# First norm on turned rows, triangular inverses through cleared images in DRAM, and a last token tile in two column halves: one encoder layer on one core

## The chip, the core and the metric

The kernel runs on one core of one Trainium2 chip. A core has a matrix engine (TensorE, PE in the profile; its weight loads are PEld), VectorE (DVE), ScalarE (ACT), GpSimd (POOL) and SyncE (SP). In this kernel SP issues every DMA, in one queue and in order; 16 DMA engines carry the transfers. The metric is the time of one execution in microseconds on the device. The kernel is written in Python against a planner: each engine's instructions are put in an order at build time, by the order of the program, by priorities, and by the planner's own estimates of when an operand will be there. Semaphores are placed from the data dependences. On the chip each engine then runs its list in that order.

## The reference

One layer of an encoder on 1024 tokens of width 1024, in float32:

```python
h = _rms_norm(x, g_mix_pre[l])
proj = h @ w_in[l]
aq, ak, av, dqkv, dgate, dalpha, dbeta = jnp.split(proj, IN_SPLITS, axis=-1)
attn_o = _window_attention(aq, ak, av, attn_sink[l])            # after rotary on aq, ak
dn_o = _gated_deltanet(dqkv, dgate, dalpha, dbeta, conv_w[l], a_log[l], dt_bias[l], g_dn_out[l])
mix = jnp.concatenate([attn_o, dn_o], axis=-1) @ w_out[l]
x = x + _rms_norm(mix, g_mix_post[l])
c = _memory_cross_attention(_rms_norm(x, g_cross_pre[l]), _rms_norm(mem, g_mem[l]), w_cq[l], w_ckv[l], w_co[l])
x = x + _rms_norm(c, g_cross_post[l])
f = _swiglu(_rms_norm(x, g_ffn_pre[l]), w_gate_up[l], w_down[l])
x = x + _rms_norm(f, g_ffn_post[l])
```

`_rms_norm` is `x * rsqrt(mean(x * x) + EPS) * gain`. In the delta net, for each of four heads and two directions, the sequence is cut into chunks; in each chunk a unit lower triangular system is solved (`triangular_solve(tmat, rhs)`, with `tmat = lower + I` from products of keys), and a scan over the chunks carries a 128x128 state.

## The kernel before

All products are done with float32 split into two parts `hi` and `lo` (`split`, L100: a cast on ScalarE, L103, and a subtraction, L104), three matmuls for each 128x128 block of weight.

**Start.** The token tiles `xts` (128 tokens each) are loaded, six of eight at first, with the gain `gmix` repeated over 128 partitions (L209) and the identity. For each tile: sum of squares on ScalarE (L222), the root by a power on POOL (`rstd_of`, L159 to L163), scaling by root and gain on VectorE (L225), eight 128x128 transposes on TensorE into two PSUM tiles (L230), and `split` of each into `hhi`, `hlo` (L232). A half of 512 tokens (`hT[hf]`) consists of four tiles. The weights of the first two projections (`ws`, L295) are asked for behind tile 1 and tile 3. `gemm_b` (L257) then does the two key projections, half by half (L297 to L300). Then come the decays' small projection (`wab`), the convolutions (L277) and the stages of `ORDER_1`, `ORDER_2` and `ORDER_3`, three lists that give the order of the program by letters: `k`, `q`, `v` are projections, `E`, `K`, `U`, `C` products of a head, `B0`, `B1` the base inverses of a group of two heads, `L0` to `L3` the levels of a head, `A`, `V`, `G` projections for attention and gates, `W` attention windows, `s01` a step of both scans.

**Base inverses and levels.** A chunk pair of 128 rows has a 128x128 triangular matrix, in four diagonal blocks of 32. `base_inverse(g)` (L521) inverts all 32x32 blocks of a group at once, one block per partition (128 partitions: 2 directions, 2 heads, 8 pairs, 4 blocks), with 60 small instructions on VectorE (L545, L547). The inverse, scaled in two ways (`A` and `V`), goes to `d_inv` (L554, four stores per group of 64 partitions, 4 KB each). `levels(h)` (L557) puts the 32x32 inverses together to inverses of 64 and 128. It loads the blocks four times as columns of blocks (`cz`, `cw`, L565), makes copies with parts of both on POOL (`m5`, `c5`, `c6`, L575 to L578), and expands these columns on VectorE to matrices that are zero outside the diagonal blocks (`D5`, `D6`, `Z0`, `Z1`, L588, a product with the mask `dmask`). `part(b)` does four pairs; both parts of a head run interleaved (`together`). The matmuls are L604 and L610, the results are stored from `Z` to `d_pz` (L629), where the scan reads them.

**End.** The last product of the feed-forward part goes over four token tiles `t` (L1774): two loads of turned activations (`atr`, L1779), their split, 33 matmuls of 512 columns into `X[t]` (L1784), an addition (L1791), sum of squares on ScalarE (`sq_of`, L1706), the root by a power on POOL (`rstd_at`, L1718 to L1723), scaling plus residual on VectorE for two column halves `za` and `zv` (L1796), and a store of each (L1797).

Of the kernel before, what the change touches and what calls it, by code (L numbers as in the profile page):

```python
# [10 lines left out]
F32 = mybir.dt.float32  # L11
# [25 lines left out]
ORDER_1 = ("k0 k1 E0 K0 U0 E1 K1 U1 S0 q0 v0 q1 C0 v1 E2 C1 k2 E3 k3 q2 K2 U2 v2 K3 U3 S1 q3 C2 v3 C3 B0 B1").split()  # L37
# [39 lines left out]
def tile_hybrid_block(  # L77
# [16 lines left out]
    def f32(ap):  # L94
        return ap.bitcast(F32)
# [69 lines left out]

    gain_at = {"cross": 60, "mem": 60 + KT, "ffn": 60 + 2 * KT}
# [16 lines left out]
    d_inv = [[dram.tile([2, 2, NT, 4, 32, 32], F32, name=f"d_inv{g}{i}") for i in range(2)] for g in range(2)]  # L183
# [19 lines left out]
    xts = [t1.tile([P, D], F32, tag="xt", name="xt", bufs=6) for _ in range(6)]  # L203
    gmix = t1.tile([P, D], F32, tag="gmix", name="gmix", bufs=1)
    xload = []
    for t in range(6):
        xload.append(nc.sync.dma_start(xts[t], x[t * P:(t + 1) * P, :]))
        if t == 0:
            nc.sync.dma_start(gmix, g_mix_pre[0].partition_broadcast(P))  # L209
            nc.sync.dma_start(ident, consts[:, 0:P])  # L210
    hT = []
    for hf in range(2):
        hi = hx.tile([P, KT, HALF], F32R, name=f"hhi{hf}")
        lo = hx.tile([P, KT, HALF], F32R, name=f"hlo{hf}")
        for j in range(4):
            t = 4 * hf + j
            xt = xts[t] if t < 6 else t1.tile([P, D], F32, tag="xt", name="xt", bufs=6)
            if t >= 6:
                nc.sync.dma_start(xt, x[t * P:(t + 1) * P, :])
# [4 lines left out]
            rstd_of(rs, ss, 1.0 / D, EPS)  # L224
            nc.vector.scalar_tensor_tensor(xt, xt, rs, gmix, ALU.mult, ALU.mult)  # L225
            for kq in range(2):
                pt = small()
                for k in range(4):
                    c = (4 * kq + k) * P
                    nc.tensor.transpose(pt[:, k * P:(k + 1) * P], xt[:, c:c + P], ident)  # L230
                o = slice(4 * kq, 4 * kq + 4), slice(j * P, (j + 1) * P)
                split(hi[:, o[0], o[1]], lo[:, o[0], o[1]], pt.rearrange("p (k t) -> p k t", k=4))  # L232
# [15 lines left out]
    nc.vector.tensor_copy(mU_r, cm["mU"])  # L248
    nc.vector.tensor_copy(mL_r, cm["mL"])
# [4 lines left out]
    nc.scalar.activation(nega, prm[:, 0:8], AF.Exp)  # L254
# [40 lines left out]
    ws = [load_w(dcols(1, h), KT, P, after=xload[t]) for h, t in ((0, 1), (1, 3))]  # L295
# [12 lines left out]
    nc.vector.tensor_scalar(wabr, hT[0][0].bitcast(F32)[:, :, 0:P], 0.0, None, ALU.mult)  # L308
# [105 lines left out]
    dmask = sm.tile([P, 4, 32], F32, name="dmask")  # L414
    nc.gpsimd.memset(dmask, 0.0)
    for q in range(4):
        nc.gpsimd.memset(dmask[32 * q:32 * q + 32, q, :], 1.0)
# [103 lines left out]
    def base_inverse(g):  # L521
# [30 lines left out]
        for i in range(2):  # L552
            for d in range(2):
                nc.sync.dma_start(d_inv[g][i][d].rearrange("h c b r s -> (h c b) r s"),  # L554
                                  (A if i == d else V)[64 * d:64 * d + 64])

    def levels(h):  # L557
# [6 lines left out]
        def fetch(dst, i, d):  # L564
            nc.sync.dma_start(dst, d_inv[g][i][d, hh].rearrange("c b r s -> (b r) c s"))  # L565

        cz = [blocks("cz0"), blocks("cz1")]
        cw = [blocks("cw0"), blocks("cw1")]
        m5, c5, c6 = blocks("m5"), blocks("c5"), blocks("c6")
        for d in range(2):  # L570
            fetch(cz[d], 1, d)
            fetch(cw[d], 0, d)
        for q in range(4):
            r = slice(32 * q, 32 * q + 32)
            nc.gpsimd.tensor_copy(m5[r], cz[1 - q % 2][r])  # L575
            nc.gpsimd.tensor_copy(c5[r], cw[q % 2][r])
        for d in range(2):
            nc.gpsimd.tensor_copy(c6[64 * d:64 * d + 64], cw[d][64 * d:64 * d + 64])  # L578
        def part(b):
# [5 lines left out]
            L5, L6, D5, D6 = wide("L5"), wide("L6"), wide("D5"), wide("D6")  # L585
            Z = [wide("Z0"), wide("Z1")]
            for e, dst, src in ((nc.vector, D5, c5), (nc.vector, D6, c6), (nc.vector, Z[0], cz[0]), (nc.vector, Z[1], cz[1])):
                e.tensor_tensor(dst.rearrange("p c (q n) -> p c q n", q=4), bc(src[:, c4, :], 2, (P, 4, 4, 32)),  # L588
                                        bc(dmask, 1, (P, 4, 4, 32)), ALU.mult)
# [24 lines left out]
            z5 = tl_.tile([P, 4, 32], F32, tag="z5", name="z5", bufs=2)  # L614
# [5 lines left out]
            mov6 = tl_.tile([P, 4, 64], F32, tag="mov6", name="mov6", bufs=2)  # L620
# [109 lines left out]
    def issue(order, table):  # L730
        for o in order:
            table[o[0]](*(int(c) for c in o[1:]))

    issue(ORDER_1, {**{n: delta_proj(n) for n in "kqv"}, "E": decays, "K": turned_keys, "U": key_products, "S": beta_rows,
                    "C": query_products, "B": base_inverse})
    pp_.close()
# [967 lines left out]
    def sq_of(src, t, ch):  # L1704
        jk = tp_.tile([P, 512], F32, tag="jk", name="jk", bufs=1)
        nc.scalar.activation(jk, src, AF.Square, accum_out=sq[:, ch, t:t + 1])  # L1706
# [63 lines left out]
    for t in range(4):  # L1770
        nc.vector.tensor_tensor(za[:, t], za[:, t], X[t], ALU.add)
        sq_of(za[:, t], 4 + t, 1)

    for t in range(4):  # L1774
        tt = slice(t * P, (t + 1) * P)
        for k0, n in ((0, 6), (6, 5)):
# [53 lines left out]
```

## Time and profile before

| | |
|---|---|
| median of 3 runs | 1531.19 us (1529.92 to 1532.13) |
| the profiled execution | 1531.03 us |
| its span from first to last instruction | 1529.3 us |
| mean granted clock of TensorE over the span | 0.994 |
| instructions | 21202 |
| DMA | 261.06 MB, 275159 packets, of them 34904 under 512 bytes |
| matmuls | 7403 |

The page gives, in this order, busy time by engine, the span in 40 slices of 38 us (one digit each, in tenths), DMA queues, the chain of work that ended last, and groups of instructions by line. In a line of a group, `out<-in x8 | 10.2, 1281 | 9.4 <-POOL rs` means 8 instructions, 10.2 us busy in all, 1281 ns each, and 9.4 us in which the engine stood idle just before them, mostly until POOL's `rs`. Lines of the view in order of time begin with start and duration in microseconds. Matmuls overlap in the pipeline, so the distance from one to the next, about 0.23 us for 512 columns, is shorter than the duration shown.

### The profile page before, as it was taken

Reading aid. Unit: us, or ns where it says so; the run is one execution under the profiler, and the core shown is the slowest. Engines: PE = TensorE matmul, PEld = TensorE weight load, DVE = VectorE, ACT = ScalarE, POOL = GpSimd, SP = SyncE. Lnnn points to the kernel's source line nnn. Section 1 sums busy time; section 2 is a strip of 40 time slices with the busy share of each in tenths; the row PEclk is TensorE's granted clock in tenths of the full one; section 3 lists DMA queues with packets and bytes.
Section 4 is the critical chain, followed back from the end, with each engine's and each line's share of the span. In section 5 each row is a group of like instructions: output and inputs, shape, how many; then the busy total and the mean of one; then the engine's idle time right before and its main releaser. Section 6 shows DMA issues by size and latency. Waiting matters only on the chain.

```text
span 1529.3 us, 21202 instructions
## 1 busy us (share of the span) xinstructions
PE 1475.7 (96%) x7403; PEld 1239.1 (81%) x7403; DVE 1116.3 (73%) x1805; ACT 752.0 (49%) x1541; POOL 364.1 (24%) x369
## 2 busy tenths in 40 slices
PE   6999999998999999999999999999999999999997
PEld 5888888877889778888788877888888888888786
DVE  6868999787888866538567768676867774696665
ACT  5578821447557764455544685223222332454532
POOL 2020221311226203252201002433534342000021
PEclk9999999999999999999999999999999999999999
DMA  6235575856987584458725554343434333853355
GB/s 208 76 109 148 144 194 142 218 176 173 322 279 236 186 296 152 141 167 271 241 97 173 192 182 134 97 138 116 146 109 153 124 103 111 321 208 97 104 177 167
DMA packets 275159, 261.06 MB, mean 171 GB/s; under 512 B 34904, under 2 KB 206829, under 8 KB 275053
## 3 DMA queue, kind: packets, MB, share of 16 engines
q1 hardware_dynamic: 275053, 259.71, 53.9%
q8 instruction: 58, 0.95, 0.3%
q14 instruction: 48, 0.39, 0.1%
HBM read 181.25 MB, written 75.79 MB: 168 GB/s over the span
## 4 chain that ended last, share of the span: by engine, by line
PE 61%; DVE 10%; DMA 10%; ACT 4%; issue 3%; SPq 2%; POOL 1%; DVEq 0%; POOLq 0%; ACTq 0%
PE pD L1481 7%; PE pE L1481 7%; PE pA L1481 6%; PE pmg L1071 6%; PE pdX L1687 6%; PE pst L1287 5%; PE pcq L262 4%; PE pB L1481 3%; PE psc L810 2%; PE pdA L1687 2%; PE pdD L1687 2%; PE pg L262 2%; DMA wraw<-in_w_gate_up_dram 1%; PE pco L1186 1%; PE pdX L1784 1%
## 5 line engine op out<-in xcount | busy, mean ns | idle before, releaser
L103 ACT CAST whi<-wraw 128x1024 fp32r<-128x1024 f32 x96 | 100.8, 1051 | 133.0 <-DMA wraw<-in_w_gate_up_dram 37.0
L262 PE MATMUL pg<-hlo,whi 128*128 128x512 f32 x352 | 139.1, 396 | 0.0
L262 PE MATMUL pg<-hhi,whi 128*128 128x512 f32 x352 | 139.1, 396 | 0.0
L262 PE MATMUL pg<-hhi,wlo 128*128 128x512 f32 x352 | 138.1, 393 | 0.0
L104 POOL TENSOR_TENSOR wlo<-wraw,whi 128x1024 fp32r<-128x1024 f32 x36 | 88.3, 2453 | 189.6 <-ACT whi L103 188.2
L1481 PE MATMUL pA<-b,whi 128*128 128x512 f32 x352 | 111.9, 400 | 3.6 <-ACT m L1508 2.8
L104 DVE TENSOR_TENSOR wlo<-wraw,whi 128x1024 fp32r<-128x1024 f32 x60 | 76.0, 1269 | 46.0 <-ACT whi L103 42.4
L1481 PEld LDWEIGHTS pA<-b,whi 128*128 128x128 f32 x352 | 66.5, 192 | 19.2 <-ACT m L1508 4.0
L1687 PE MATMUL pdX<-dhl,whi 128*128 128x512 f32 x264 | 76.1, 390 | 1.5 <-ACT dhl L103 0.8
L262 PEld LDWEIGHTS pg<-hhi,whi 128*128 128x128 f32 x352 | 66.3, 189 | 13.4 <-ACT hhi L103 0.2
L262 PEld LDWEIGHTS pg<-hhi,wlo 128*128 128x128 f32 x352 | 66.2, 188 | 12.8
L262 PEld LDWEIGHTS pg<-hlo,whi 128*128 128x128 f32 x352 | 66.2, 188 | 12.7
L1564 POOL TENSOR_TENSOR act<-act,up 128x512 f32<-128x512 f32 x33 | 50.7, 1538 | 83.1 <-DVE up L1563 61.8
L1481 PE MATMUL pA<-b,wlo 128*128 128x512 f32 x176 | 69.9, 398 | 0.5 <-DVE wlo L104 0.5
L103 ACT CAST whi<-araw 128x1024 fp32r<-128x1024 f32 (+1 forms) x36 | 35.3, 982 | 67.9 <-PE pdX L1687 27.6
L104 DVE TENSOR_TENSOR wlo<-araw,whi 128x1024 fp32r<-128x1024 f32 (+1 forms) x36 | 40.9, 1135 | 36.1 <-ACT whi L103 35.7
L1536 POOL TENSOR_TENSOR sr<-wraw 128x512 f32<-128x512 f32 x22 | 30.3, 1379 | 150.7 <-DMA wraw<-in_w_gate_up_dram 98.7
L287 DVE SCALAR_TENSOR_TENSOR acc<-cp,cols,acc 128x1024 f32<-128x1024 f32 x48 | 62.1, 1297 | 0.1
L1687 PEld LDWEIGHTS pdX<-dhl,whi 128*128 128x128 f32 x264 | 49.3, 188 | 12.7 <-ACT dhl L103 1.1
L1721 POOL TENSOR_SCALAR frs<-sq 128x1 f32<-128x1 f32 x8 | 11.9, 1497 | 194.5 <-ACT jk L1706 193.6
L103 ACT CAST dhl<-b 128x512 fp32r<-128x512 f32 x66 | 40.3, 620 | 31.6 <-PE pdA L1687 13.7
L1481 PE MATMUL pB<-s0h,s1h 128*128 128x512 f32 x176 | 54.5, 391 | 0.0
(484 smaller groups left out, 4285.5 us busy)
## 6 DMA issues: line engine op xcount, KB each, us to landing
wraw<-in_w_gate_up_dram SPq DMA_DIRECT2D x54, 512.0 KB, 3.9
kv<-d_kv SPq DMA_DIRECT2D x32, 512.0 KB, 7.5
wraw<-in_w_in_dram SPq DMA_DIRECT2D x22, 512.0 KB, 4.2
b<-in_w_down_dram SPq DMA_DIRECT2D x20, 512.0 KB, 8.0
araw<-d_as SPq DMA_DIRECT2D x20, 512.0 KB, 3.7
pz<-d_pz SPq DMA_DIRECT2D x32, 256.0 KB, 7.6
wraw<-in_w_ckv_dram SPq DMA_DIRECT2D x16, 512.0 KB, 6.3
wraw<-in_w_out_dram SPq DMA_DIRECT2D x16, 512.0 KB, 3.7
```

The lines of the kernel that those rows point to most:

```text
L103: nc.scalar.copy(hi, src)
L104: return (eng or nc.vector).tensor_tensor(lo, src, f32(hi), ALU.subtract)
L262: nc.tensor.matmul(p_, w[:, k, :], ah[a][:, k, :], start=(k == 0 and i == 0), stop=(k == nk - 1 and i == 2))
L287: nc.vector.scalar_tensor_tensor(acc, cp[:, t:t + S], taps[t], acc, ALU.mult, ALU.add)
L810: nc.tensor.matmul(out[:, d, h, :], lt[:, d, h, :], rt[:, d, h, :], start=True, stop=True)
L1071: nc.tensor.matmul(pp[t], act[a][:, k, tt], w_[:, kk, :], start=(k == 0 and i == 0), stop=(k == KT - 1 and i == 2))
L1186: nc.tensor.matmul(po, vr_[a][:, kt, cs], pts[kt][b_], start=(kt == 0 and i == 0), stop=(kt == 1 and i == 2))
L1287: nc.tensor.matmul(bank, a[:, tt], w, start=(start and i == 0), stop=(stop and i == 2), skip_group_check=not check)
L1481: nc.tensor.matmul(out_, w[a][:, k, :], xx[b_][:, k, :], start=(start and k == 0 and i == 0), stop=(k == HK - 1 and i == 2), skip_group_ch ...
L1536: nc.gpsimd.tensor_tensor(s[0], b_[:, 0:HK], b_[:, HK:], ALU.add)
L1564: nc.gpsimd.tensor_tensor(o_, o_, up, ALU.mult)
L1687: nc.tensor.matmul(banks[t], a[:, k - k0, tt], w, start=(first and k == 0 and i == 0), stop=(k == NB - 1 and i == 2), skip_group_check=not ...
```

## The change

Three parts, independent of each other.

1. The gain is loaded as 8 rows of 128 (4 KB), turned once on TensorE to a column per block (`gcol`), and multiplied where the turned block is cast (ScalarE, by `scale=g`) and cut (VectorE). Scaling of a token tile is by its root alone. All eight token tiles have buffers of their own and are loaded first; the first two weights are queued on SP behind tile 3, their casts and subtractions behind tile 3's root and scaling, and behind the sixth turned block. A PSUM tile now holds one block column `k` of four token tiles instead of four columns of one. Roots are a Sqrt on ScalarE and a reciprocal on VectorE, its table loaded at the start by `warm`. Some small copies and the Exp for `nega` are queued behind the last scaling and the last root.
2. `d_inv` is replaced by `d_lv`, for each group an image of 16 matrices of 128 rows by 512 columns (four matrices side by side: `D5`, `D6`, `Z0`, `Z1`). It is cleared from a tile of zeros by four DMAs of 1 MB per group, at the letters `Z` in `ORDER_1`; `base_inverse` stores its blocks on the diagonals, and `levels` loads four images at once (1 MB, `DZ`, three buffers). `m5` goes through a small tensor `d_m5`. The columns, copies, masks and expansions go. `z5` and `mov6` get one buffer instead of two.
3. Roots of the last four tiles are on ScalarE and VectorE too. The last tile's 33 matmuls of 512 columns become 33 of the first 256 columns and 33 of the last 256, the latter in a PSUM tile of their own; additions, squares and stores follow by halves.

```diff
-ORDER_1 = ("k0 k1 E0 K0 U0 E1 K1 U1 S0 q0 v0 q1 C0 v1 E2 C1 ...
+ORDER_1 = ("k0 k1 Z E0 Z K0 Z U0 Z E1 K1 U1 S0 q0 Z v0 Z q1 Z C0 Z v1 E2 C1 ...
+    def inverse_root(rs, ss, scale, bias):
+        root = nc.scalar.activation(rs, ss, AF.Sqrt, bias=bias, scale=scale)
+        nc.vector.reciprocal(rs, rs)
+        return root
-    d_inv = [[dram.tile([2, 2, NT, 4, 32, 32], F32, name=f"d_inv{g}{i}") for i in range(2)] for g in range(2)]
+    LW, LB_ = 4 * P, 32 * 4 * P + 32
+    d_lv = [dram.tile([1, 8 * NT * LB_ + LW], F32, name=f"d_lv{g}") for g in range(2)]
+    d_m5 = [dram.tile([8 * NT, 32, 32], F32, name=f"d_m5{g}") for g in range(2)]
+    def diagonal(g, kind):
+        at = kind * P
+        return (d_lv[g][0, at:at + 8 * NT * LB_].rearrange("(n y) -> n y", y=LB_)[:, 0:32 * LW]
+                .rearrange("n (r w) -> n r w", w=LW)[:, :, 0:32])
+    def level_rows(g, x0):
+        return (d_lv[g][0, 0:8 * NT * LB_].rearrange("(x y) -> x y", y=4 * LB_)[x0:x0 + 4, 0:P * LW]
+                .rearrange("x (p w) -> p x w", w=LW))
...
-    xts = [t1.tile([P, D], F32, tag="xt", name="xt", bufs=6) for _ in range(6)]
-    gmix = t1.tile([P, D], F32, tag="gmix", name="gmix", bufs=1)
+    xts = [t1.tile([P, D], F32, tag="xt", name="xt", bufs=NT) for _ in range(NT)]
+    grow = t1.tile([KT, P], F32, tag="grow", name="grow", bufs=1)
+    gcol = t1.tile([P, KT], F32, tag="gcol", name="gcol", bufs=1)
...
-            nc.sync.dma_start(gmix, g_mix_pre[0].partition_broadcast(P))
+            nc.sync.dma_start(grow, g_mix_pre[0].rearrange("(c p) -> c p", p=P))
             nc.sync.dma_start(ident, consts[:, 0:P])
+    warm = t1.tile([P, 1], F32, tag="ss", name="warm", bufs=4)
+    nc.scalar.activation(warm, epsc, AF.Sqrt)
+    pt = small()
+    nc.tensor.transpose(pt[:, 0:KT], grow, ident[0:KT, 0:KT])
+    nc.vector.tensor_copy(gcol, pt[:, 0:KT])
...
-            rstd_of(rs, ss, 1.0 / D, EPS)
-            nc.vector.scalar_tensor_tensor(xt, xt, rs, gmix, ALU.mult, ALU.mult)
-            for kq in range(2):
...
+            rooted = inverse_root(rs, ss, 1.0 / D, epsc)
+            scaled = nc.vector.tensor_scalar(xt, xt, rs, None, ALU.mult)
+        if hf == 0:
+            ready.append((rooted, scaled))
+        for k in range(KT):
+            pt = small()
+            for j in range(4):
+                nc.tensor.transpose(pt[:, j * P:(j + 1) * P], xts[4 * hf + j][:, k * P:(k + 1) * P], ident)
+            g = gcol[:, k:k + 1]
+            cast = nc.scalar.activation(hi[:, k, :], pt, AF.Identity, scale=g)
+            cut = nc.vector.scalar_tensor_tensor(lo[:, k, :], pt, g, f32(hi[:, k, :]), ALU.mult, ALU.subtract)
+            if hf == 0 and k == 5:
+                ready.append((cast, cut))
...
-    ws = [load_w(dcols(1, h), KT, P, after=xload[t]) for h, t in ((0, 1), (1, 3))]
+    ws = []
+    for h in range(2):
+        with tc.issue_after(ready[h][0].ins), tc.issue_after(ready[h][1].ins):
+            ws.append(load_w(dcols(1, h), KT, P, after=xload[3]))
...
+    def clear():
+        g, x0 = cleared[0] // 4, 4 * (cleared[0] % 4)
+        cleared[0] += 1
+        nc.sync.dma_start(level_rows(g, x0), bc(zero, 1, (P, 4, LW)))
...
-        for i in range(2):
-            for d in range(2):
-                nc.sync.dma_start(d_inv[g][i][d].rearrange("h c b r s -> (h c b) r s"),
-                                  (A if i == d else V)[64 * d:64 * d + 64])
+        for d in range(2):
+            first, second = (A, V) if d == 0 else (V, A)
+            lo_, hi_ = 64 * d, 64 * d + 64
+            nc.sync.dma_start(d_m5[g][1 - d::2], second[lo_ + 1 - d:hi_:2])
+            nc.sync.dma_start(diagonal(g, 0)[d::2], first[lo_ + d:hi_:2])
+            nc.sync.dma_start(diagonal(g, 2 + d), second[lo_:hi_])
+            for q in (2 * d, 2 * d + 1):
+                nc.sync.dma_start(diagonal(g, 1)[q::4], first[lo_ + q:hi_:4])
...
+        m5 = blocks("m5")
+        nc.sync.dma_start(m5, d_m5[g][32 * hh:32 * hh + 32].rearrange("(c b) r s -> (b r) c s", b=4))
...
-            L5, L6, D5, D6 = wide("L5"), wide("L6"), wide("D5"), wide("D6")
-            Z = [wide("Z0"), wide("Z1")]
-            for e, dst, src in ((nc.vector, D5, c5), (nc.vector, D6, c6), (nc.vector, Z[0], cz[0]), (nc.vector, Z[1], cz[1])):
-                e.tensor_tensor(dst.rearrange("p c (q n) -> p c q n", q=4), bc(src[:, c4, :], 2, (P, 4, 4, 32)),
-                                        bc(dmask, 1, (P, 4, 4, 32)), ALU.mult)
+            L5, L6 = wide("L5"), wide("L6")
+            DZ = tl_.tile([P, 4, 4, P], F32, tag="DZ", name="DZ", bufs=3)
+            nc.sync.dma_start(DZ.rearrange("p c k n -> p c (k n)"), level_rows(g, hh * NT + 4 * b))
+            D5, D6, Z = DZ[:, :, 0], DZ[:, :, 1], [DZ[:, :, 2 + d] for d in range(2)]
...
+    nc.vector.tensor_tensor(zv[:, 3, 256:], zv[:, 3, 256:], X[3][:, 256:], ALU.add)
+    XL = bank("pdY")
...
+        columns = [(slice(0, 512), X[t])] if t < 3 else [(slice(0, 256), X[t][:, 0:256]), (slice(256, 512), XL[:, 0:256])]
+        for c_, p_ in columns:
+            fresh = c_.start > 0
+            for k, (ah, al) in enumerate(tiles):
                 for i, (a, w) in enumerate(((ah, t4h), (ah, t4l), (al, t4h))):
+                    nc.tensor.matmul(p_, a, w[:, k, c_], start=(fresh and k == 0 and i == 0), stop=(k == NB - 1 and i == 2),
+                                     skip_group_check=not fresh)
...
+        known = sq[:, 1, r:r + 1]
+        nc.vector.tensor_scalar(known, known, D * EPS, None, ALU.add)
+        for c_, p_ in columns:
+            nc.vector.tensor_tensor(zv[:, t, c_], zv[:, t, c_], p_, ALU.add)
+            sq_of(zv[:, t, c_], r, 0)
+            nc.vector.tensor_tensor(zv[:, t, c_], zv[:, t, c_], gp[:, c_], ALU.mult)
+            if c_.stop < 512:
+                nc.vector.tensor_tensor(known, known, sq[:, 0, r:r + 1], ALU.add)
+        rs = tp_.tile([P, 1], F32, tag="frs", name="frs")
+        inverse_root(rs, sq[:, 0, r:r + 1], 1.0, known)
+        for z, o_, c_ in [(za, 512, slice(0, 512))] + [(zv, 0, c_) for c_, _ in columns]:
+            at = slice(o_ + c_.start, o_ + c_.stop)
+            nc.vector.scalar_tensor_tensor(z[:, t, c_], z[:, t, c_], rs, xr[:, at], ALU.mult, ALU.add)
+            nc.sync.dma_start(out[there(r), at], z[:, t, c_])
```

70 lines of the change are left out of this document (21 added, 49 removed).

## The prediction

> **What bounds the kernel now.** I read the page's first two parts and its chain first, then busy time by stretch, then the first 30 us and the last 10 us in order of time, and last the groups of the operations that the change touches.
>
> ```profile
> PE 1475.7 (96%) x7403; PEld 1239.1 (81%) x7403; DVE 1116.3 (73%) x1805; ACT 752.0 (49%) x1541; POOL 364.1 (24%) x369
> PE   6999999998999999999999999999999999999997
> PE 61%; DVE 10%; DMA 10%; ACT 4%; issue 3%; SPq 2%; POOL 1%; DVEq 0%; POOLq 0%; ACTq 0%
> ```
>
> TensorE is the bound: it stands below 9 tenths in the first slice, the last one, and one slice near 345 us. The change takes no matmul away (it adds one small transpose and splits 33 others in two), so it can win only where TensorE stands still. How much that is:
>
> ```profile
> 0.00:8.00 8.00, 0.00 (x0) 0.00 (x0) 1.28 (x1) 2.43 (x3) 2.04 (x20) 1.00 0.78 239
> 8.00:24.70 16.70, 10.85 (x50) 8.44 (x50) 14.02 (x18) 13.85 (x25) 8.32 (x12) 1.00 0.82 266
> 24.70:47.80 23.10, 23.10 (x113) 19.31 (x112) 15.99 (x28) 11.33 (x19) 0.74 (x2) 1.00 0.28 81
> ...
> 180.00:220.00 40.00, 40.00 (x211) 34.02 (x209) 39.02 (x59) 15.06 (x47) 8.39 (x9) 1.00 0.64 164
> 220.00:260.00 40.00, 37.60 (x205) 31.35 (x204) 36.90 (x79) 8.11 (x18) 11.49 (x20) 1.00 0.65 159
> 260.00:300.00 40.00, 38.98 (x211) 32.93 (x211) 27.99 (x54) 13.30 (x27) 12.51 (x21) 1.00 0.84 220
> 300.00:340.00 40.00, 38.59 (x222) 32.80 (x219) 33.96 (x78) 20.60 (x54) 6.37 (x9) 1.00 0.66 188
> 340.00:400.00 60.00, 53.45 (x364) 47.71 (x363) 43.87 (x120) 39.10 (x86) 10.03 (x12) 1.00 0.72 214
> ```
>
> Columns: stretch, its length, busy us and count of PE, PEld, DVE, ACT, POOL, clock, DMA share, GB/s. PE has nothing for 8 us, half a load until 24.7 us, and then no gap (47.86, quoted below, is the last matmul of the first two projections). From 180 to 400 us, where the levels and the start of the scan lie, it is idle 0 + 2.40 + 1.02 + 1.41 + 6.55 = 11.4 us in all, with VectorE close to full in the first two stretches. These are the three places: start, levels, tail.
>
> **Part 1, the first norm.** What it is now, in order of time and by groups:
>
> ```profile
> 1.24 0.42 SPq L209 DMA_DIRECT2D gmix<-in_g_mix_pre_dram  x1
> ...
> 2.65 0.43 SPq L125 DMA_DIRECT2D wraw<-in_w_in_dram  x1
> ...
> 4.48 1.06 ACT L222 ACTIVATE junk<-xt 128x1024 f32<-128x1024 f32 x1 [2.41 <-DMA xt<-in_x_dram]
> ...
> 12.73 1.06 ACT L222 ACTIVATE junk<-xt 128x1024 f32<-128x1024 f32 x1
> ...
> 16.12 4.03 PE L230 MATMUL ps<-ident,xt 128*128 128x128 f32 x16 [2.33 <-DVE xt L225]
> ...
> 21.74 1.07 PE L230 MATMUL ps<-ident,xt 128*128 128x128 f32 x8 [0.55 <-DVE xt L225]
> ```
> ```profile
> 47.86 0.39 PE L262 MATMUL pg<-hhi,wlo 128*128 128x512 f32 x1
> ```
> ```profile
> L285 ACT ACTIVATE acc<-pg,cols 128x512 f32<-128x512 f32 x24 | 16.8, 699 | 0.0
> ...
> L225 DVE SCALAR_TENSOR_TENSOR xt<-xt,rs,gmix 128x1024 f32<-128x1024 f32 x8 | 10.2, 1281 | 9.4 <-POOL rs L163 9.2
> ...
> L103 ACT CAST hhi<-ps 128x512 fp32r<-128x512 f32 x16 | 8.7, 582 | 1.6 <-PE ps L230 1.6
> ...
> L928 DVE TENSOR_SCALAR mt<-mt,mrs 128x1024 f32<-128x1024 f32 x2 | 1.5, 754 | 1.2 <-POOL mrs L163 1.2
> L222 ACT ACTIVATION_READ_ACCUMULATOR junk<-xt 128x1 f32 x8 | 1.5, 187 | 0.0
> ...
> L222 ACT ACT_TABLE_LOAD x1 | 1.3, 1283 | 0.8 <-PEq L1816 0.8
> ```
> ```profile
> L1310 ACT ACTIVATE prs<-ssq 128x1 f32<-128x1 f32 x8 | 2.3, 289 | 0.1
> ...
> L1311 DVE RECIPROCAL prs<-prs 128x1 f32<-128x1 f32 x8 | 0.9, 147 | 0.6 <-ACT prs L1310 0.6
> ```
>
> Now: between the squares of tile 0 (4.48) and tile 3 (12.73) lie 8.25 us, in which the gain's 512 KB, ident's 64 KB, tile 1, a weight tile (issued at 2.65), tile 2 and tile 3 come in: 5.125 units of 512 KB, 1.61 us each. After: the gain is 4 KB, and both weight loads are issued behind tile 3, so 3.125 units, 5.03 us: tile 3 at 9.5. If a weight tile's pieces still mix in, 11.1. I take 10.0, nearer to the first because the order of issue is the one that the row of tile 0 obeys.
>
> Then for tile 3: square 1.06, read 0.19, root 0.29, reciprocal 0.15, scaling 0.75 (the row of L928, the same form, for L225's 1.28) and some 0.15 of hand-overs: 2.6, so all four tiles are scaled at 12.6. Only now can a group of four turned blocks be finished. TensorE will already have turned tiles 0 to 2 in the five free PSUM buffers: 15 blocks of 64.
>
> What had TensorE done by 24.7? 48 blocks at 1.07/8 = 0.134 and two matmuls of 0.23: 6.9 us of work at its later speed. After the change 15 x 0.134 = 2.0 is done at 12.6. The rest needs 4.9, and more because the array starts slow: blocks took 4.03/16 = 0.25 at 16.12 and 0.134 at 21.74, after 4 to 5.6 us without a stop. Half speed over some 5 us loses 2.5. So 12.6 + 4.9 + 2.5 = 20.0 stands against 24.7: 4.7 us earlier. From it I take 0.7, for the first weight's cast (1.05), which now must follow tile 3's root and meets the first turned cast on ScalarE. Bounds: 2 (tile 3 at 11.1, the full 1.05, slow for one us more) and 5.5 (tile 3 at 9.5, no collision).
>
> The Trainium skill (TensorE: Matmul & The Clock Gate, Part 4: PE-mode transpose) says that transposes do not count as activity for the clock gate. By that rule the array would stay slow until plain matmuls have filled the start, and the gain would be about 2 us smaller. The trace speaks against it: blocks ran slow from 16.12 and fast from 21.74, with hardly more than three plain matmuls between.
>
> What ScalarE gets besides: 8 roots of 0.29, 16 casts at 0.70 instead of 0.58, and one more table load of 1.28 for the Exp behind the last root: 5.5 us. Hidden: from tile 3's arrival it has two weight casts (2.1), 16 casts (11.2), four squares with reads (5.0) and four roots (1.2), so it ends at about 29.5, while TensorE has the first half's 32 blocks and 48 matmuls, 15.2 us, until some 28. Without that cover it would cost up to 2 us. VectorE saves 8 x 0.53 less 8 x 0.15; POOL's powers go; neither bounds. Moving the small constants' copies behind the last scaling (L248, L308) delays work that is first needed near 48 us. Term: **-4.0** (-5.5 to -2).
>
> **Part 2, the matrix images.**
>
> ```profile
> L588 DVE TENSOR_TENSOR Z<-cz,dmask 128x512 f32<-128x512 f32 x16 | 11.3, 724 | 7.3 <-DMA d_pz<-Z 7.0 <-DMA cz<-d_inv 0.3
> L588 DVE TENSOR_TENSOR D<-c,dmask 128x512 f32<-128x512 f32 x16 | 11.2, 713 | 1.0 <-POOL c L576 1.0
> ```
> ```profile
> d_inv<-A SPq DMA_DIRECT2D x4, 256.0 KB, 3.8
> cz<-d_inv SPq DMA_DIRECT2D x8, 128.0 KB, 3.2
> ```
>
> Removed: 32 expansions, 22.5 us of VectorE, the 7.0 us it waited there for the stores of Z, POOL's copies, and 16 loads of 128 KB in pieces of 128 bytes. Added: 8 clears of 1 MB, per head group ten stores (1.25 MB, nearly all in pieces of 128 bytes), per head two loads of 1 MB and one of 128 KB. SP issues 40 DMAs where it issued 24.
>
> The gain: VectorE, 39.0 of 40 and 36.9 of 40 us full where both base inverses and the first levels run, loses 22.5 us of work. It cannot return more than TensorE's 11.4 us of gaps. Much of these is latency (the scan's first steps, the rope's moves), so I take 3; from 0 to 8.
>
> The cost: the DMA share leaves 14.4 + 14 + 6.4 + 13.6 + 16.8 = 65 us free from 180 to 400. The 8 MB of image loads at what 260:300 shows (220 GB/s at 0.84, so 262 when full) need 32 us. They fit in all, but not in 260:300, where 6.4 is free and two heads' images take 16. A transfer that slips there delays a level or the rope, and with it TensorE by a part of that: I take 2, from 0 to 10. The clears come where the share is low (0.28 in 24.7:47.8); each holds the engines for 4 us, behind which a weight load waits, and that load is asked for one projection (48 matmuls, 11 us) ahead: nothing, unless several clears come at once (then 2 us each beyond the third).
>
> The wait for Z's stores does not vanish: with three image buffers for eight parts, five image loads wait for the stores of the part three before, now on SP, and behind them in its one queue stand the rope's moves, windows' loads and weights. It was 7.0 us in all on VectorE, and a weight load's 11 us of cover holds each piece of it. One buffer for z5 and mov6 adds a hand-over per part, hidden behind projections. Term: **-1.0** (-8 to +10).
>
> **Part 3, the tail.**
>
> ```profile
> 1461.19 30.18 PE pdX L1687 x132
> ...
> 1514.57 7.34 PE pdX L1784 x31
> ...
> 1521.93 0.70 DVE zv L1791
> ...
> 1522.71 0.63 ACT jk L1706
> ...
> 1523.53 0.80 POOL frs L1721
> ...
> 1525.01 0.75 DVE za L1796
> 1525.76 0.66 DVEq L1825
> ```
> ```profile
> 475.31 1.67 PE pck L950 x14
> ```
>
> From the last matmul's end (1521.91) to the span's end (1529.3) are 7.4 us. After, only 256 columns are left behind the last matmul: add about 0.42 (half of 0.70 with some fixed part), square and read 0.42 + 0.19 - 0.1, root 0.29, reciprocal 0.15, three scalings at 0.66 + 0.39 + 0.48, hand-overs 0.3, and the last store, now 1529.3 - 1526.42 = 2.9: 6.1, or 1.3 less. The matmuls of the last tile: 33 at 30.18/132 = 0.229 become 66 at 1.67/14 = 0.119: +0.3. The second group of its turned activations is needed after 18 half matmuls instead of 18 whole ones, 2 us earlier, which costs up to 0.5 (I take 0.1). One table load (1.28) comes in a gap of ScalarE three tiles earlier. Term: **-0.9** (-1.4 to +0.3).
>
> **Sum.** -4.0 - 1.0 - 0.9 = -5.9. The profiled execution took 1531.03 (span 1529.3 and 1.7 around it), 0.16 under the median 1531.19, so 1525.1 and, by the median, 1525.3: I say **1525**.
>
> **The rivals.**
>
> *The stores become the wait* (slower). The ten stores of a group go to interleaved rows of one DRAM tensor. If each waits for the one before to land, 10 x 3.2 = 32 us pass in SP's queue, against some 5 for the four of now, and every weight load stands behind. Cover is one projection, 11 us; group 0's images have six projections before their result is needed, group 1's have the scan close behind. Price: 27 - 11 = 16 once, so 1525 + 16 - 2 = 1539. It decides from 16 us between first issue and last landing. For it: the row cz shows 128 KB in small pieces taking nearly as long (3.2) as 256 KB in whole rows (3.8). Against it: other stores into interleaved places of one tensor (d_pz) are issued back to back today.
> The Trainium skill (DMA: Bandwidth & Descriptors, Specifications) gives 512 bytes as the least for full rate and says that below it the engine reads, modifies and writes. That points the same way; the trace has small pieces only as reads, so no row shows it for stores.
>
> *The start gains little.* Every group of blocks now needs all four tiles; if a weight tile slips ahead of tile 3 and ScalarE is late by its 5.5 us, -0.5 is left of the 4: 1529. For it: ScalarE is busy 13.85 of 16.7 us there already.
>
> *VectorE was the bound of the levels.* Then 8 of the 11.4 us return and nothing slips: 1518. For it: 39.02 of 40. Against it: TensorE had no gap at all in that very stretch.
>
> **How the numbers follow.** Forecast 0.42 (by itself 1521 to 1528.5), stores 0.24, start 0.18, VectorE 0.16. No change, within 0.2%, is 1528.1 to 1534.3. Faster: 0.39 of the forecast, 0.16 and 0.06 of the start's case, 0.61. Slower: 0.20 of the stores' case and 0.02 of the start's, 0.22. The rest, 0.17, within. The range from 1516 to 1538 leaves out the ends of the two outer cases.
>
> **What would show it.** Start: the square of tile 3 near 10, turned blocks without a break from 12 to 13, the first two projections' last matmul (L262, 47.86 now) near 44. Levels: PE's idle time from 180 to 400 near 10 us; stores of a group landed within 12 us of the first issue. Tail: 6 us from last matmul to end. The forecast is wrong if TensorE's first unbroken run starts after 22, if SP's weight loads show waits on the image's stores, or if a gap above 3 us stands before the scan.

## The result: slower by 1.5%, and the profile after

| | before | after |
|---|---|---|
| median of 6 runs | 1530.73 us (1528.84 to 1532.13) | 1555.66 us (1546.82 to 1558.60) |
| the profiled execution, its span | 1531.03, 1529.3 | 1557.15, 1555.4 |
| mean granted clock of TensorE | 0.994 | 0.98 |

The ratio is 1.0154 (95% interval 1.0127 to 1.0181): 25 us slower where 1525 had been forecast. The page of the profile after has its busy row and its slices changed in one place:

```profile
PE 1490.4 (96%) x7437; PEld 1255.1 (81%) x7437; DVE 1093.4 (70%) x1795; ACT 757.9 (49%) x1556; POOL 329.3 (21%) x301
...
PE   7999998898799889999999999999999999999998
PEclk9999999897899989999999999999999999999999
```

VectorE has indeed less to do (1093.4 us, 1116.3 before). But where TensorE had one slice below 9 between the first and the last, it now has six, all in the first 583 us, and the clock falls in the same part. Busy time by stretch shows the place (columns as in the prediction: stretch, length, PE, PEld, DVE, ACT, POOL, clock, DMA share, GB/s):

```profile
8.00:24.70 16.70, 14.63 (x60) 11.08 (x60) 13.21 (x23) 16.01 (x32) 0.00 (x0) 1.00 0.83 277
...
220.00:260.00 40.00, 40.00 (x180) 33.08 (x180) 35.66 (x73) 7.26 (x10) 2.08 (x2) 1.00 0.49 134
260.00:300.00 40.00, 31.05 (x155) 25.98 (x154) 15.79 (x35) 6.28 (x14) 2.78 (x3) 0.87 0.93 250
300.00:340.00 40.00, 38.07 (x204) 33.25 (x204) 22.72 (x62) 24.57 (x59) 4.27 (x5) 0.91 0.64 198
340.00:400.00 60.00, 53.77 (x313) 47.16 (x312) 41.48 (x109) 34.08 (x91) 7.83 (x12) 0.83 0.64 191
400.00:440.00 40.00, 32.43 (x231) 30.73 (x231) 27.40 (x72) 19.08 (x41) 10.81 (x6) 0.87 0.96 290
```

The start is better (14.63 busy where 10.85 was). From 220 to 260 TensorE is full, fuller than before (37.60), then it falls to 31.05 (38.98 before) and, from 400 to 440, to 32.43 (38.99). From 260 to 440 the clock is 0.83 to 0.91, where it was 1.00 in all these stretches before; between 300 and 400 TensorE is as busy as before, but at the lower clock. Full first and empty later reads as projections done early, with nothing left to put between the levels. Why the levels were not there shows in SP's queue, in order of time (start, duration, line, destination and source):

```profile
254.69 0.48 SPq L591 DMA_DIRECT2D d_m<-V  x1
255.22 0.66 SPq L593 DMA_DIRECT2D d_lv<-V  x1
...
262.55 1.36 SPq L595 DMA_DIRECT2D d_lv<-V  x1
...
266.55 0.37 SPq L605 DMA_DIRECT2D m<-d_m  x1
266.97 1.57 SPq L615 DMA_DIRECT2D DZ<-d_lv  x1
268.59 0.97 SPq L618 DMA_DIRECT2D Ul<-d_u  x1
```

and before:

```profile
215.74 0.36 SPq L510 DMA_DIRECT2D d_pz<-pm  x1
...
216.91 0.58 SPq L565 DMA_DIRECT2D cz<-d_inv  x1
```

Head 0 needs group 0's inverse, whose ten stores went out from 196.8 to 206.3 in the kernel after. Yet its first loads are issued at 266.55, behind the last store of group *1* (V, 262.55): 50 us later than `cz` before. The view of waits names that store for head 0's first load, L605 (0.8 us in all, once, 0.8 at the longest), although the load reads only what group 0 stored:

```profile
SPq L605 <- DMA d_lv<-V: 0.8, 1, 0.8
```

TensorE pays at once:

```profile
267.70 0.39 PE L289 MATMUL pg<-hhi,wlo 128*128 128x512 f32 x1
276.08 1.11 PE L622 MATMUL ps<-ident,Ul 128*128 128x128 f32 x4 [7.99 <-DMA Ul<-d_u]
...
277.42 0.63 PE L289 MATMUL pg<-hlo,whi 128*128 128x512 f32 x1
277.85 0.63 PE L289 MATMUL pg<-hhi,wlo 128*128 128x512 f32 x1
...
281.13 0.39 PE L289 MATMUL pg<-hlo,whi 128*128 128x512 f32 x1
281.36 0.39 PE L289 MATMUL pg<-hhi,wlo 128*128 128x512 f32 x1
```

8.4 us from one matmul to the next, and then matmuls 0.43 us apart until 281, where 0.23 is the rate on both sides. The Trainium skill (TensorE: Matmul & The Clock Gate, Part 1: The HAM clock gate) says that the gate knows full and half speed only and falls back when the array has idled; these rows agree, 0.43 against 0.23.

Some points of the lists, read from the rows in order of time (us), for nine of the kernels. "Projections" is the last matmul of the first two; "levels" are the first turned `Ul` of head 0 and the last product of head 3; "scan" is its first matmul:

| run | projections | head 0's first load | levels from | to | scan |
|---|---|---|---|---|---|
| before | 47.9 | 216.9 | 223.6 | 356.9 | 365.7 |
| after | 43.0 | 266.5 | 276.1 | 385.9 | 395.7 |
| e1, before + tile in t2 | 47.7 | 253.4 | 260.8 | 388.0 | 395.3 |
| e9, before + tile elsewhere | 47.9 | 216.7 | 223.5 | 356.4 | 365.2 |
| e2, after, tile elsewhere | 42.7 | 214.8 | 222.4 | 363.6 | 370.9 |
| e3, part 1 alone | 41.4 | 213.9 | 221.7 | 359.7 | 372.4 |
| e5, part 2 alone, tile elsewhere | 48.3 | 221.7 | 229.7 | 369.9 | 381.1 |
| e10, e2 + pm on GpSimd | 41.8 | 228.2 | 237.0 | 376.2 | 386.7 |
| e16, e2 + two buffers | 43.3 | 216.0 | 224.4 | 359.3 | 377.6 |

Between before and after, the scan starts 30.0 us later, and the last matmul ends 27 us later. The rest of the kernel only carries this to the end.

### The profile page after: what moved, and what is told of

It reads as the page before. It is cut to its first block, busy times and chain, and to the rows that moved or that the text cites. A ratio compares the mean times of both kernels' runs of the same rounds, so it can differ in the third digit from the quotient of the medians.

```text
span 1555.4 us, 21253 instructions
## 1 busy us (share of the span) xinstructions
PE 1490.4 (96%) x7437; PEld 1255.1 (81%) x7437; DVE 1093.4 (70%) x1795; ACT 757.9 (49%) x1556; POOL 329.3 (21%) x301
## 4 chain that ended last, share of the span: by engine, by line
PE 65%; DMA 8%; DVE 7%; SPq 3%; ACT 2%; issue 2%; POOL 0%; DVEq 0%; ACTq 0%; POOLq 0%
PE pD L1509 8%; PE pE L1509 8%; PE pA L1509 6%; PE pmg L1099 6%; PE pdX L1715 6%; PE pst L1315 5%; PE pcq L289 4%; PE pdA L1715 4%; PE pB L1509 4%; PE psc L838 3%; PE pdD L1715 2%; DMA wraw<-in_w_ckv_dram 2%; PE pg L289 2%; PE pco L1214 1%; PE pdX L1819 1%
## 5 line engine op out<-in xcount | busy, mean ns | idle before, releaser
L1509 PE MATMUL pE<-s0l,bhi 128*128 128x512 f32 x176 | 54.2, 389 | 0.0
```

The source lines that it names most:

```text
L1509: nc.tensor.matmul(out_, w[a][:, k, :], xx[b_][:, k, :], start=(start and k == 0 and i == 0), stop=(k == HK - 1 and i == 2), skip_group_ch ...
```

## The experiments

Theory: nothing that the change computes is to blame, but the place of its tile of zeros. `zero` (2 KB per partition) was put into the pool `t2`; the pools lie one behind another, so everything above it moves up by 2 KB, among it the V of the second group. The levels' pool takes the same memory once the earlier pools are closed, and its first tiles then lie on that V, which is free only when group 1's stores have landed (the pools' order is in the kernel; the wait of L605 above fits it). Rival: the traffic of the images (clears, small pieces, 1 MB loads).

### The tile alone, and the change without its place

**e1**: the kernel before, with a tile that nothing reads.

```diff
+    pad = t2.tile([P, 512], F32, tag="pad", name="pad", bufs=1)
+    nc.gpsimd.memset(pad, 0.0)
```

> The kernel before with nothing but a cleared tile of 2 KB per partition more, in the pool t2, where the change put its tile of zeros; nothing reads it, all that is computed stays. Placement theory: the tile moves the second group's V up over the first tiles of the levels, so head 0's block loads (cz, cw) start only behind group 1's last d_inv store (near 255 instead of 217), TensorE runs out of projections, and the time is 10 to 28 us above the kernel before (1541 to 1558), with cz's first load at 250 or later. Rival (the images' DMA traffic is the cost): no image is here, so the time is the kernel before's within 2 us, 1529 to 1533.

Measured: 1560.75 us, ratio 1.0204 (1.0182 to 1.0227), 31 us slower, with no image, no clear and no larger load. The size is 3 us above what was written; the mechanism is there in SP's queue:

```profile
252.04 1.19 SPq L556 DMA_DIRECT2D d_inv<-A  x2
253.38 0.57 SPq L567 DMA_DIRECT2D cz<-d_inv  x1
```

`cz` of head 0 now follows group 1's last store (216.91 before).

**e9**, the control: the same tile, cleared in the same way, in a pool above both V.

```diff
+    pad = pp_.enter_context(pool("tz", 1)).tile([P, 512], F32, name="pad")
+    nc.gpsimd.memset(pad, 0.0)
```

> The kernel before with the same cleared tile of 2 KB as in the run with the tile in t2, but in a pool of its own above both V; nothing reads it. Placement theory: nothing lies on another address, every engine runs the same list as before, so 1526 to 1533, within 0.2% of the kernel before. Rival (2 KB less of free memory, or the clearing itself, is what costs): 1550 or more.

Measured: 1530.11 us, ratio 1.0006 (0.9991 to 1.0020). The queue is as before:

```profile
216.75 0.58 SPq L567 DMA_DIRECT2D cz<-d_inv  x1
```

So neither 2 KB less of memory nor the clearing costs anything; the address does.

**e2**: the whole change, with only the tile of zeros moved.

```diff
-    zero = t2.tile([P, LW], F32, tag="zero", name="zero", bufs=1)
+    zero = pp_.enter_context(pool("tz", 1)).tile([P, LW], F32, name="zero")
```

> The changed kernel with only the tile of zeros moved to a pool of its own, above both V. Same clears, stores, loads. Placement theory: head 0's m5 and first image loads start before group 1's stores (near 215 to 220), no TensorE gap above 3 us before 300, granted clock 1.00 from 260 to 340, and 1518 to 1530 in all. Rival (the image traffic and the loads' own time are the cost): 1545 or more, with head 0's images late by their landing.

Measured: 1528.58 us, ratio 0.9993 (0.9978 to 1.0007) to the kernel before. The same images, stores and loads, and some 25 us are gone (0.9993 where the ratio was 1.0154; the medians differ by 27):

```profile
214.78 0.57 SPq L605 DMA_DIRECT2D m<-d_m  x1
215.45 0.56 SPq L615 DMA_DIRECT2D DZ<-d_lv  x1
```
```profile
220.00:260.00 40.00, 37.59 (x198) 31.83 (x199) 33.76 (x81) 6.50 (x16) 0.16 (x1) 0.96 0.73 211
260.00:300.00 40.00, 34.08 (x176) 28.27 (x175) 18.94 (x40) 15.43 (x36) 4.66 (x4) 0.92 0.93 241
...
340.00:400.00 60.00, 55.33 (x351) 49.34 (x350) 39.99 (x103) 36.70 (x84) 9.06 (x11) 0.94 0.74 243
```

The placement theory's first load holds; what it said of gaps and clock does not quite (3.2 us of TensorE ahead of the first `Ul`, clock 0.92 from 260 to 300), and the forecast's gain of 6 us is not there either. That is the second question.

### The parts, each alone

**e3** is part 1 alone, **e4** part 3 alone, **e5** part 2 alone with the tile in its own pool, **e6** parts 2 and 3: the diff of the change, cut to these parts.

> The kernel before with part 1 alone (gain on turned blocks, token tiles first, ScalarE's roots there); inverses and tail as before. If the start's gain stays (as in the changed kernel's trace, where the first projections ended some 6 us earlier): 1523 to 1527. Rival: the gain is given back where the levels wait for VectorE's base inverses, because the projections only run out earlier: 1528 to 1532, with larger TensorE gaps from 220 to 400.

> The kernel before with part 3 alone (last token tile in column halves, roots of the last four tiles on ScalarE and VectorE). If the term of the prediction holds: 0.9 us below the kernel before, about 1530 (1529.2 to 1531). If the stalls that the changed kernel's trace shows ahead of and inside the last tile come with this part, they eat the 1.3 us behind the last matmul: 0 to +1.5 us.

> The kernel before with part 2 alone, the tile of zeros in a pool of its own above both V. Theory (the images relieve VectorE, and the start's lead was lost because group 0's base inverse ended 9 to 11 us later, 192.7 and 194.5 instead of 183.5): without the start that inverse ends at 184 to 186 again, group 1's at 245 to 260 instead of 269.9, and the time is 1520 to 1527. Rival (the images cost what they save; the 11 us between the start alone and the changed kernel with the tile moved are the order's luck): 1528 to 1534.

> Parts 2 and 3 without part 1, the tile of zeros in its own pool. Theory: 1 to 2 us below part 2 alone, 1518 to 1526, and so below the kernel with all three parts and the tile moved (1528.6). Rival (the start's gain is real at the end as well): above it.

Measured: e3 1539.60 us (ratio 1.0061, 1.0039 to 1.0083); e4 1528.10 (0.9993, 0.9983 to 1.0002); e5 1543.76 (1.0106, 1.0077 to 1.0134); e6 1542.58 (1.0098, 1.0070 to 1.0127). Both theories fell, and e3 and e5 lie above every range that was written. The start alone is 9 us *slower* although its projections end 6.5 us earlier, the images alone are 16 us slower, and both together cost nothing. The tail is worth about 1 us each time (e4; e6 against e5), near the edge of what can be told.

In e3 group 0's base inverse ends at 192.6 instead of 183.5. VectorE's groups between its first and last step, e3 first, then before:

```profile
L301 DVE SCALAR_TENSOR_TENSOR acc<-cp,cols,acc 128x1024 f32<-128x1024 f32 x19 | 25.1, 1322 | 0.4 <-ACT acc L299 0.4
...
L527 DVE TENSOR_TENSOR pm<-pc,C 128x512 f32<-128x512 f32 x8 | 5.3, 689 | 0.0
```
```profile
L287 DVE SCALAR_TENSOR_TENSOR acc<-cp,cols,acc 128x1024 f32<-128x1024 f32 x16 | 20.4, 1273 | 0.0
...
L509 DVE TENSOR_TENSOR pm<-pc,C 128x512 f32<-128x512 f32 x4 | 2.7, 688 | 2.1 <-DMA d_pz<-pm 2.1
```

In e3 the planner put more query products and convolutions between the inverse's 60 steps. That became the next theory: the late inverse takes the lead back. (e5 already spoke against it: there the inverse ended at 183.5, as before, and the run was 16 us slower all the same.)

**e7**: group 0's inverse ahead of all query products; **e10**: the masked products `pm` on GpSimd, which leaves VectorE 11 us more.

```diff
-ORDER_1 = ("k0 k1 Z E0 Z K0 Z U0 Z E1 K1 U1 S0 q0 Z v0 Z q1 Z C0 Z v1 E2 C1 k2 E3 k3 q2 K2 U2 v2 K3 U3 S1 q3 C2 v3 C3 B0 B1").split()
+ORDER_1 = ("k0 k1 Z E0 Z K0 Z U0 Z E1 K1 U1 S0 B0 q0 Z v0 Z q1 Z C0 Z v1 E2 C1 k2 E3 k3 q2 K2 U2 v2 K3 U3 S1 q3 C2 v3 C3 B1").split()
+    def query_products(h):
+        with tc.issue_after(inverted[0].ins):
+            query_products_(h)
```
```diff
-                nc.vector.tensor_tensor(pm, pc, bc(cm[mi], 1, (P, 4, P)), ALU.mult)
+                nc.gpsimd.tensor_tensor(pm, pc, bc(cm[mi], 1, (P, 4, P)), ALU.mult)
```

> All three parts with the tile of zeros moved, and group 0's base inverse ahead of the query products of every head (B0 behind S0 in the order, query products placed behind its last scaling). Theory (the late base inverse of group 0 takes back the start's lead): its last subtraction ends by 184 instead of 194.5, head 0's levels follow some 10 us earlier, and the time is 1519 to 1526. Rival (that inverse is not what the scan waits for; the work pushed behind it, 11 instructions of 0.7 us, comes back ahead of group 1's inverse): 1526 to 1531, the scan's first matmul no earlier than 369.

> All three parts with the tile of zeros moved, and the 16 masked products pm (128x512, 0.69 us each on VectorE, 11 us in all) on GpSimd. Theory (VectorE, full from 100 to 220, is what holds back the last query products and the base inverses, and so takes the start's lead): group 0's base inverse ends 3 to 8 us earlier than 194.5, head 0's levels start 3 to 6 us earlier than 222.35, and the time is 1519 to 1526. Rival (GpSimd is slower, 1.3 to 2.4 us a piece by its other products, and the masked products come late in SP's queue): 1528 to 1536.

Measured: e7 1570.35 us (1.0282, 1.0235 to 1.0329), e10 1549.12 (1.0128, 1.0104 to 1.0151). The inverse did end at 166.8 and at 183.7, earlier than e2's 194.5, and it helped in neither; both lie above every range that was written. In e7 TensorE's list then had a query product next, which now stood behind the inverse, and waited for it 10.6 us:

```profile
169.45 1.19 PE L513 MATMUL ps<-gm,mL_r 128*128 128x512 f32 x2 [10.62 <-DVE pc L548]
```

In e10 VectorE stood, and TensorE behind it:

```profile
208.91 2.07 DVE L572 SCALAR_TENSOR_TENSOR A<-V,bB 64x1024 f32<-64x1024 f32 x1 [8.99 <-DMA b<-d_beta]
```
```profile
224.11 1.12 PE L480 MATMUL ps<-ident,acc 128*128 128x128 f32 x4 [9.09 <-ACT acc L315]
```

So the late inverse is not *the* cause. But the VectorE row names a new wait: group 1's beta rows, 8 KB, stand on SP behind group 0's ten stores. e5 has it too, and the kernel before does not (no idle time in brackets):

```profile
202.15 1.97 DVE L554 SCALAR_TENSOR_TENSOR A<-V,bB 64x1024 f32<-64x1024 f32 x1 [4.41 <-DMA bB<-d_beta]
```
```profile
196.60 2.07 DVE L536 SCALAR_TENSOR_TENSOR A<-V,bB 64x1024 f32<-64x1024 f32 x1
```

### The beta rows ahead of the stores

**e12** (on e5), **e13** (on e2) and **e11** (on e10) gave group 1's beta rows buffers of their own, 256 bytes per partition, and issued the loads of such rows early (those of both groups). These buffers were put beside the tile of zeros:

```diff
-        bB = tb.tile([P, 32], F32, tag="bB", name="bB", bufs=1)
-        b1 = tb.tile([64, 32], F32, tag="b1", name="b1", bufs=1)
+        bB = (tz0 if g else tb).tile([P, 32], F32, tag="bB", name="bB", bufs=1)
+        b1 = (tz0 if g else tb).tile([64, 32], F32, tag="b1", name="b1", bufs=1)
...
+        with tc.high_priority(AHEAD):
+            for d in range(2):
+                nc.sync.dma_start(bB[64 * d:64 * d + 64], bv[d])
+            nc.sync.dma_start(b1, bv[1])
```

> Part 2 alone with the tile of zeros moved, and group 1's beta rows (bB, b1) in buffers of their own, loaded ahead of group 0's ten stores instead of behind them. Theory (VectorE's stall of 4.41 us ahead of L554 at 202.15, and the query products behind it, are what part 2 loses: small loads queued on SP behind the stores): no VectorE stall over 2 us between 185 and 215, head 0's turned Ul at 224 to 227 instead of 229.7, and 1535 to 1540 against 1543.8. Rival (the levels lose by the images' loads and hand-overs whenever they start): 1541 or more.

> All three parts with the tile of zeros moved, and group 1's beta rows ahead of group 0's stores. With the tile moved VectorE showed no stall there (none over 1 us from 180 to 230), so the theory of the late beta rows expects nothing from it: 1526 to 1531. If the planner puts group 1's base inverse earlier for it, its last subtraction comes ahead of 258.8 and the time at 1520 to 1526.

> As the run with the masked products on GpSimd, and group 1's beta rows in buffers of their own, ahead of group 0's ten stores. Theory (the 8.99 us in which VectorE waits for b1 ahead of L572 at 208.91, and TensorE's gap of 9.25 us at 214.6 behind it, are those loads queued behind the stores): both gaps under 3 us, head 0's turned Ul at 226 to 230 instead of 237, and 1538 to 1543 against 1549. Rival (GpSimd's masked products at 1.7 us each are the late ones): 1546 or more.

Measured: 1562.94, 1560.63 and 1581.28 us, all three 19 to 32 us slower than what they started from, where every expectation had said faster or the same. It was the first mistake over again. The zeros are free after the clears, but the beta rows live until group 1's inverse is scaled, and the levels' tiles lie on them. In e12:

```profile
271.91 2.59 SPq L579 DMA_DIRECT2D d_lv<-V  x2
274.55 0.63 SPq L589 DMA_DIRECT2D m<-d_m  x1
```

**e14** (on e5) and **e15** (on e2) put the same 256 bytes into `sm`, where nothing of the levels lies; the diff is the one above with `sm` for `tz0`.

> Part 2 alone with the tile of zeros moved, and group 1's beta rows in the pool sm, where nothing of the levels lies on their addresses, loaded ahead of most of group 0's stores. Placement theory for the run with these rows in the tile of zeros' pool (1563, levels behind group 1's inverse): here the levels start ahead of group 1's stores again and the time is below 1550. Theory of the late beta rows: 1535 to 1540 against 1543.8. Rival (the stall only moves to the next store: A is rewritten for group 1 when its own four stores have landed, as in the 6.47 us in that run): 1541 to 1548.

> All three parts, tile of zeros moved, group 1's beta rows in sm ahead of group 0's stores. Placement theory: the levels start near 222 again and not at 273, so the time is near the kernel with the tile moved, 1524 to 1532, and not 1560. Rival (the early beta rows themselves cost): 1545 or more.

Measured: e14 1546.26 us (1.0108, 1.0089 to 1.0127), e15 1531.29 (1.0015, 1.0002 to 1.0027). The levels start early again, so place is shown a third time, with 256 bytes. The beta rows, on the other hand, were not what part 2 loses: e14 is no faster than e5, because the stall only moves on to the stores themselves (`A` is one buffer for both groups, so group 1 may write it only when group 0's stores from it have landed; the row names the store that came last):

```profile
205.76 2.07 DVE L555 SCALAR_TENSOR_TENSOR A<-V,bB 64x1024 f32<-64x1024 f32 x1 [6.27 <-DMA d_lv<-V]
```

### Inside the levels

**e8** issues `Ul` (256 KB) ahead of the image (1 MB); **e16** gives `z5` and `mov6` two buffers again. Both are on e2.

```diff
+            Ul = wide("Ul")
+            nc.sync.dma_start(Ul, d_u[g][hh, c4].rearrange("c p n -> p c n"))
             nc.sync.dma_start(DZ.rearrange("p c k n -> p c (k n)"), level_rows(g, hh * NT + 4 * b))
...
-            Ul = wide("Ul")
-            nc.sync.dma_start(Ul, d_u[g][hh, c4].rearrange("c p n -> p c n"))
```
```diff
-            z5 = tl_.tile([P, 4, 32], F32, tag="z5", name="z5", bufs=1)
+            z5 = tl_.tile([P, 4, 32], F32, tag="z5", name="z5", bufs=2)
-            mov6 = tl_.tile([P, 4, 64], F32, tag="mov6", name="mov6", bufs=1)
+            mov6 = tl_.tile([P, 4, 64], F32, tag="mov6", name="mov6", bufs=2)
```

> All three parts with the tile of zeros moved, and in each part of a head the load of Ul (256 KB) issued ahead of the image (1 MB) instead of behind it. Theory (TensorE's 3.16 us gap at 218.8 is Ul queued behind the image): that gap is under 1 us, head 0's turned Ul start 3 us earlier than 222.35, and the time is 1524 to 1528. Rival (the levels' own pace and not their start sets the scan): 1527 to 1531.

> All three parts, tile of zeros moved, z5 and mov6 in two buffers as before the change. If the single buffers make the levels slow (with the tile moved they take 141 us from the first turned Ul to the last product, 133 before): 133 to 137 there and 1522 to 1527. Rival (the hand-over between the two parts of a head is covered by projections, as the prediction had it): 139 to 143 there and 1527 to 1531.

Measured: e8 1535.63 us (1.0050, 1.0031 to 1.0069), e16 1537.02 (1.0051, 1.0033 to 1.0069). In e8 the levels began at 220.4 instead of 222.4, and TensorE's gap only moved to 216.9 (3.0 us). In e16 they took 134.9 us instead of 141.2, as the theory had it, and still the scan began 6.6 us later: after the last level product (359.3) TensorE did 18 us of other work that the list puts first. Both runs lie above every range that was written. A faster pace of the levels alone therefore brought nothing. That the scan never waits for them is not shown: in the kernel before and in e2 it begins only some 9 and 7 us behind their last product.

## Why the prediction was wrong, point by point

- **The bound and the gaps.** Right, but used in one direction only. 11.4 us of gaps is the most that could be *won* between 180 and 400; nothing in those rows limits what could be lost, and the range's upper end, 1538, came from the priced cases alone.
- **Part 1.** Locally right and a little better than said: the square of tile 3 at 10.48 (forecast 10), matmuls from 14.23 on, last projection at 43.04 (forecast 44):

```profile
10.48 1.04 ACT L243 ACTIVATE junk<-xt 128x1024 f32<-128x1024 f32 x1
```
```profile
43.04 0.39 PE L289 MATMUL pg<-hhi,wlo 128*128 128x512 f32 x1
```

  That is -4.8 where the term said -4.0. What failed here is the sum, which carried a lead won by 48 us through to the end. With the tile moved (e2) 5.2 us of lead were 1.3 when the levels began and -5.2 at the scan; alone (e3) it ended 9 us behind. One reading on the way has rows against it: that turned blocks with hardly a plain matmul bring the array to full rate. Now fifteen blocks ran from 10.24 to 14.3 without a gap, 4.06/15 = 0.27 us each, and the matmuls behind them were still 0.42 us apart (16.53 to 16.95). Full rate, 0.24 apart, came at 18.4, some 4 us behind the first plain matmul at 14.23.
- **Part 2.** This is the step that failed. The list of what is added names clears, stores and loads, and leaves out the tile that the clears are made from, so its place was put at nothing, without a reason. This tile is the 25 us: +31 by itself (e1), gone when it is moved (e2), nothing when it lies elsewhere (e9).
- **The slip of transfers (+2, 0 to +10), the hand-overs ("hidden behind projections").** With the place put right, part 2 alone is 16 us slower, outside the term's +10. Two of its waits were seen: VectorE ahead of group 1's inverse, 4.4 to 6.3 us behind ten stores (e5, e14), and TensorE's 3.2 us for `Ul` (e2). The single buffers of `z5` and `mov6` did slow the levels, by 6.3 us (e2 against e16), though taking them back did not help the end. VectorE's relief was real (in e2 it is busy 18.94 from 260 to 300 instead of 27.99) and bought nothing.
- **The stores become the wait.** Not as priced: group 1's ten went out in 9.2 us and the last had landed by 266.5, 12 us after the first issue, under the 16 at which it was to decide. The weight load behind them was issued at 265.26, before that. In smaller form, on VectorE, it came true in e5.
- **The start gains little.** The end was right (e3, worse even), the reason wrong: TensorE's start did gain.
- **VectorE was the bound of the levels.** Wrong as far as these runs show: VectorE was relieved of 22.5 us, in e10 of 11 more, and no run was faster for it. (e5 and e10 have new waits of VectorE on transfers, 4.41 and 8.99 us, so neither is a clean test.)
- **The tail.** 6.1 us from the last matmul to the end were forecast, and it is 1555.4 - 1549.24 = 6.2:

```profile
1548.96 0.28 PE L1819 MATMUL pdY<-t4h,wlo 128*128 128x256 f32 x1
```

  As a whole e4 gives -1.1 us with an interval that reaches just past zero, beside -0.9.
- **The signs named** did their work: a gap above 3 us before the scan was to prove the forecast wrong, and it stood at 267.70.

What stays open: no single wait explains why parts 1 and 2 each lose 9 to 16 us and together nothing. The parts are independent in what they compute, but not in time. Every edit of this stage makes the planner write other lists for all engines, and most runs with such an edit came out 7 to 20 us above the run that they started from (e3, e5, e8, e10, e16; e7 more; but e14 and e15 by under 3), while e9, whose lists are those of before, moved by less than can be measured. That the lists' order is the cause is argued from this, not shown. No version was found that beats the kernel before by more than the spread; e2, at its level, beats the changed one by 25 to 27 us. That e2's parts cancel was not foreseen: it is luck, and no support for the sum.

## What to carry to other kernels

A buffer costs its place as well as its bytes: before adding one to a kernel whose memory is reused by stages, find out whose addresses move and until when the old owner lives, and read the first load of the next stage for a wait that its data do not need. A gain at the start need not be a gain at the end of a kernel whose lists are tuned as a whole, so test a part alone and follow its lead from point to point. An upper bound on a gain, from the idle time of the busiest engine, is no bound on a loss.

## What the runs showed of the hardware that was not expected

Stores in pieces of 128 bytes to interleaved DRAM rows cost rate, but did not become the wait. The view of transfers of the kernel after, from 195 to 210 us (destination and source, count, KB each, us from issue to landing):

```profile
d_lv<-A SPq DMA_DIRECT2D x1, 128.0 KB, 4.1
d_lv<-A SPq DMA_DIRECT2D x2, 64.0 KB, 3.1
```

That is about the 3.8 us of 256 KB in whole rows before, for a half and a quarter of the bytes. From 197 to 206 us, where 6128 of 6690 packets were under 512 bytes, the 16 transfer engines were busy for a share of 0.81 and moved 145 GB/s. From 190 to 196, with 96 of 2968 under that size, the same share moved 245. The rule on pieces under 512 bytes that the prediction quoted from the Trainium skill (DMA: Bandwidth & Descriptors, Specifications) agrees with that rate; that these stores are read, modified and written again is not shown by any row.

The granted clock made the gaps dearer: from 340 to 400 it was 0.83. If there are a full and a half speed only, as the matmuls 0.23 and 0.43 us apart say, a third of that stretch ran at half speed. TensorE was busy in 53.77 of its 60 us there, hardly other than the 53.45 of before, but a matmul at half speed counts as busy for longer: 313 instructions where there were 364. No single wait of TensorE in that stretch is longer than 1.61 us, so the half speed did not need a long standstill.
